# Turning the softmax rows by VectorE and a way through memory instead of by TensorE

## The chip, the cores and the metric

The kernel runs on one core of one Trainium2 chip. Its time is the device time of one execution in microseconds; a kernel's figure is the median of its runs. Beside the times there is one profiled execution, recorded instruction by instruction, from which all rows quoted here come. TensorE (PE, with its weight loads PEld) multiplies matrices, VectorE (DVE), ScalarE (ACT) and GpSimd (POOL) work on tiles, SyncE (SP) issues DMAs. The matrices pass through TensorE as float32r pairs: each operand is split into a high part and a low part (the rest), and a product is made of two or three matmuls.

## The reference, cut to what matters

One encoder block over 512 positions of width 2048. An adaLN-modulated RMSNorm gives `h`; one projection of `h` feeds 16 attention heads of width 64 and a gated linear attention (GLA); both are gated, concatenated and projected back.

```
h = rms_norm(x) * (1 + scale) + shift
proj = h @ w_in                       # q, k, v, gate of attention; q, k, v, gate, decay of GLA
for window, dilation in ((128, 1), (512, 4), (2048, 16)):
    s = q k^T / 8 + bias              # masked to the pattern
    o_p, lse_p = softmax(s) v, logsumexp(s)
att = sum_p softmax(lse)_p * o_p      # = one softmax over all positions, with a bias that counts
                                      #   how many patterns a pair of positions lies in
```

As the last comment says, the three patterns together are one softmax over the 512 keys with another bias, and that is how the kernel computes it: for each head and each tile of 128 queries a row block of scores 128 x 512, its softmax P, and P v. For P v TensorE needs P with the keys in the partitions, so P (queries in the partitions) has to be turned.

## The kernel before, in words

The weights stream through memory once, in groups of 512 KB (`fetch`, buffers `raw`), are split into parts by ScalarE (`split_hi`, L313) and VectorE (`split_lo`, L297), and are multiplied with `h` in *units* of 512 columns. A unit (`unit`) issues 64 steps ("ticks") of three matmuls each (L169 to L171, 512 columns wide): 8 weight groups of 8 ticks. Between the ticks stands side work, given as a list of pairs (place from 0 to 1, function); what has a place of 1 or more spills into the next unit. The order of TensorE's instructions is that of the program. The instructions of the other engines are laid into their queues by a scheduler, which looks at readiness and priority; each queue then runs strictly in its order.

Attention is side work of four units: qk2, qk4, qk6 and gk. Each takes four heads with four query tiles each, 16 score tiles (`attention`). For one tile `score` multiplies queries with keys (two matmuls, L576 and L577), VectorE adds the bias row and takes the minimum (L580), ScalarE exponentiates with a row sum (L583), VectorE inverts the sum (L584), GpSimd scales the row (L585). Two items later `turn` transposes the tile by four TensorE transposes into PSUM (L597), and ScalarE and VectorE read the high and the low part of P^T from there (L601, L602). When the two tiles of a half (256 queries) are turned, `values` makes eight matmuls with them (L611), ScalarE copies half of the result (L614) and VectorE adds the other (L618). At the end of each qk unit `qk_evict` moves the new queries and keys out of PSUM (L539 to L551), with DMAs that copy between partition halves.

Score tiles, softmax rows, queries and keys share 16 buffers of one kind (`T2`); the parts of P^T share eight larger ones (`B8`) with other tensors; PSUM tiles of attention share three banks (`PA`). The loads of weights use four buffers (`RAW`).

Two units of attention also carry `some_sums`: multiply-and-sum passes of VectorE over matrices that are loaded for that (L680, L244), which later units carry too.

Of the kernel before, what the change touches and what calls it, by code (L numbers as in the profile page):

```python
# [18 lines left out]
P = 128  # L19
# [50 lines left out]

ATT_AT = (0.17, 0.8, 0.04, 0.05, 0.05)

GLA_AT = (0.01, 0.02, 0.33, 0.46, 0.46, 0.56, 0.64, 0.76, 0.76, 0.88)
GLA_FIRST = 0.2

SUMS_IN = {"qk6": 4, "gk": 4, "gv0": 9, "gv1": 2, "ag0": 7, "ag1": 9, "gg0": 9}


def _plan(tasks, free, ready):
# [52 lines left out]
def block_kernel(ctx: ExitStack, tc: tile.TileContext, a: dict):  # L134
# [21 lines left out]
    def PA(name):  # L156
        return pp.tile([P, 512], F32, tag="pa", bufs=3, name=name)
# [47 lines left out]
    def RAW(name, shape):  # L205
        return wp.tile([P] + shape, F32, tag="raw", bufs=4, name=name)
# [349 lines left out]
    def attention(pairs):  # L556

        tiles = [(2 * p + j, i) for p in pairs for j in range(2) for i in range(4)]
        gt, pt, pr_ = {}, {}, {}
        heads = [2 * p + j for p in pairs for j in range(2)]  # L560

        def g_load(h):
# [4 lines left out]
        def score(h, i):  # L567
            def go():
                if h % 8 == 0 and i == 0:
                    cat[h // 8] = B8(f"cat{h // 8}", [4, 512])  # L570
                if i == 1 and h != heads[-1]:
                    g_load(h + 1)
                qs, ks, kl, _ = stacks[h]
                q = slice(P * i, P * i + P)
                ps = PA(f"s{h}{i}")
                mm(ps, qs[:, q], ks, start=True, stop=False)  # L576
                mm(ps, qs[:, q], kl, start=False, stop=True)  # L577
                t = T2(f"p{h}{i}")
                st = sm.tile([P, 3], F32, tag="st", name=f"st{h}{i}", bufs=6)
                nc.vector.tensor_tensor_reduce(  # L580
                    out=t, in0=ps, in1=gt[h][:, P * i:P * i + 512], op0=ALU.add, op1=ALU.min,
                    scale=1.0, scalar=3e38, accum_out=st[:, 0:1])
                act(t, t, AF.Exp, bias=st[:, 0:1], scale=-1.0, accum_out=st[:, 1:2])  # L583
                nc.vector.reciprocal(st[:, 2:3], st[:, 1:2])  # L584
                nc.gpsimd.tensor_scalar(t, t, st[:, 2:3], 1.0, op0=ALU.mult, op1=ALU.mult)  # L585
                pr_[h, i] = t
            return go

        def turn(h, i):
            def go():  # L590
                half, ii = divmod(i, 2)
                if ii == 0:
                    pt[h, half] = B8(f"pt{h}{half}", [2, 4, 256], F32R)
                t = pr_.pop((h, i))
                pk = PA(f"t{h}{i}")
                for kt in range(4):
                    nc.tensor.transpose(pk[:, kt * P:kt * P + P], t[:, kt * P:kt * P + P], ident)  # L597
                hi = pt[h, half][:, 0, :, P * ii:P * ii + P]
                lo = pt[h, half][:, 1, :, P * ii:P * ii + P]
                src = pk.rearrange("p (k q) -> p k q", k=4)  # L600
                act(hi, src, AF.Copy)  # L601
                tt(lo, src, hi.bitcast(F32), op=ALU.subtract)  # L602
            return go
# [16 lines left out]

        items = []
        n = len(tiles)
        for x in range(n + 4):
            if x < n:
                items.append(score(*tiles[x]))
            if 2 <= x <= n + 1:
                items.append(turn(*tiles[x - 2]))
            if 3 <= x <= n + 2 and tiles[x - 3][1] % 2 == 1:
                items.append(values(tiles[x - 3][0], tiles[x - 3][1] // 2))
        g_load(heads[0])  # L630
        start, span, move0, move1, move_last = ATT_AT
        at = [start + (q + 0.5) / len(items) * span for q in range(len(items))]
        at[0] -= move0
        at[1] -= move1
        at[-1] += move_last
        return list(zip(at, items))

    def gate_half(m, z):

# [203 lines left out]
    def unit(name, natural, side=(), rhs=None, lr=None, tiles=range(4)):  # L843
# [5 lines left out]
        for q in range(KT // 2):  # L849
# [3 lines left out]
            if 0 in tiles:  # L853
                todo = list(range(gi[name, gorder[0] if name == "o3" else 0], upto[name, g] + 1))
                for i in todo:
                    split_hi(i)
                for ahead in (1, 2):
                    fetch(upto[name, g] + ahead)
            if i0 not in low:
                split_lo(i0)  # L860
# [270 lines left out]
```

## Time and profile before

| | us |
|---|---|
| median of 3 runs | 958.21 |
| lowest, highest run | 958.14, 959.61 |
| profiled execution | 959.9 |
| its span in the trace | 957.9 |

The span is the time from the first to the last recorded instruction; 2.0 us of the execution lie around it. In the groups of instructions, a row names the line, the engine, the operation, the tiles written and read, the shapes and the count; then the busy time and the mean of one in ns; then how long the engine stood idle just before them, and what ended that. A helper's line stands for all that call it. In the answers in order of time, a row gives the start, the duration, the engine and the instruction, and in brackets the idle time before it. In the chain of work that ended last, a row gives the start, the time that the chain spent on the instruction, and the instruction; "issue" is time in which nothing recorded was waited for. In DMA rows stand the size of one and the median time from issue to landing.

### The profile page before, as it was taken

The page shows a single profiled execution, that of the slowest core. Times are in us where ns is not written, and L with a number is a line of the kernel's source. Part 1 is how long each engine was busy: PE and PEld are TensorE (multiplying, and loading weights), DVE is VectorE, ACT ScalarE, POOL GpSimd, SP SyncE. Part 2 cuts the span into 40 slices and gives each one's busy share as a digit, 9 for nine tenths or more (in the row PEclk, how much of TensorE's full clock was granted, in tenths as well). Part 3 has the DMA queues.
Part 4 walks back from the last instruction along what each step waited for, and adds up shares of the span by engine and source line. Part 5 has one row for each costly group of instructions (what it writes and reads, how often), then busy time and mean ns, then how long its engine had stood idle before and what let it go on. Part 6 is the DMA issues. An engine that isn't in the chain of part 4 may idle for free.

```text
span 957.9 us, 11999 instructions
## 1 busy us (share of the span) xinstructions
PE 939.7 (98%) x4464; PEld 777.1 (81%) x4464; DVE 605.3 (63%) x900; ACT 431.5 (45%) x719; POOL 81.1 (8%) x100
## 2 busy tenths in 40 slices
PE   8999999999999999999999999999999999999996
PEld 5888788888888888888778888888887888888884
DVE  7988899675756676766435656675964352546421
ACT  5443533565655655655215544543834152233222
POOL 0000000012122022122000000000010000202120
PEclk9999999999999999999999999999999999999998
DMA  9999687443333463533454244354555464244013
GB/s 330 413 411 365 229 296 275 150 131 105 112 103 105 144 200 108 173 127 103 150 176 146 86 132 154 132 176 154 173 195 183 132 221 154 92 151 152 23 55 121
DMA packets 45180, 163.76 MB, mean 171 GB/s; under 512 B 5730, under 2 KB 6018, under 8 KB 40386
## 3 DMA queue, kind: packets, MB, share of 16 engines
q1 hardware_dynamic: 44946, 162.68, 49.9%
q8 instruction: 35, 0.57, 0.2%
q10 hardware_dynamic: 176, 0.33, 0.1%
q14 instruction: 23, 0.18, 0.1%
HBM read 154.51 MB, written 4.28 MB: 166 GB/s over the span
## 4 chain that ended last, share of the span: by engine, by line
PE 84%; DMA 6%; DVE 5%; issue 3%; ACT 1%; SPq 0%; POOL 0%; ACTq 0%; DVEq 0%; POOLq 0%
PE ps_o L170 6%; PE ps_o L169 6%; PE ps_o L171 6%; DMA rawg<-in_wg 6%; PE ps_qk L170 5%; PE ps_qk L169 5%; PE ps_qk L171 5%; PE o L611 3%; PE sta L169 3%; PE sta L170 3%; PE sta L171 3%; PE stb L171 3%; PE stb L169 3%; PE stb L170 3%; PE ps_gv L171 3%; PE ps_gv L170 3%
## 5 line engine op out<-in xcount | busy, mean ns | idle before, releaser
L585 POOL TENSOR_SCALAR p<-p,st 128x512 f32<-128x512 f32 x64 | 45.5, 711 | 406.6 <-DVE st L584 357.9
L244 DVE CUSTOM_DVE_ANT_0 cb<-cb,sb,c_bcond 128x2048 f32<-128x2048 f32 (+1 forms) x32 | 73.4, 2294 | 0.0
L583 ACT ACTIVATE p<-p,st 128x512 f32<-128x512 f32 x64 | 46.1, 721 | 56.8 <-DVE st L580 56.3
L602 DVE TENSOR_TENSOR pt<-t,pt 128x512 fp32r<-128x512 f32 x64 | 44.0, 689 | 16.2 <-ACT pt L601 15.8
L580 DVE CUSTOM_DVE_ANT_0 p<-s,g 128x512 f32<-128x512 f32 x64 | 43.6, 687 | 14.8 <-PE s L577 14.5
L601 ACT ACTIVATE pt<-t 128x512 fp32r<-128x512 f32 x64 | 37.8, 592 | 10.2 <-PE t L597 9.2
L244 DVE CUSTOM_DVE_ANT_0 rawg<-rawg,sb,gate 128x1024 f32<-128x1024 f32 x16 | 20.5, 1283 | 29.6 <-DMA rawg<-in_wg 29.6
L611 PEld LDWEIGHTS o<-pt,vv 128*128 128x128 f32 x256 | 34.7, 188 | 5.0 <-DVE pt L602 2.2
L597 PEld LDWEIGHTS t<-c_ident,p 128*128 128x128 f32 x256 | 31.8, 140 | 8.5
L597 PE MATMUL t<-c_ident,p 128*128 128x128 f32 x256 | 38.3, 272 | 0.0
L611 PE MATMUL o<-pt,vv 128*128 128x256 f32 x256 | 36.6, 283 | 0.9 <-DVE pt L602 0.8
L244 DVE CUSTOM_DVE_ANT_0 rawg<-rawg,sb,c_bcond 128x1024 f32<-128x1024 f32 x16 | 20.5, 1283 | 26.3 <-DMA rawg<-in_wg 26.3
L1014 POOL TENSOR_TENSOR x<-x,fgain 128x512 f32<-128x512 f32 x12 | 20.3, 1696 | 185.3 <-ACT ysq L1012 185.3
L1012 ACT ACTIVATE ysq<-x 128x512 f32<-128x512 f32 x16 | 10.1, 632 | 47.2 <-DVE x L1010 47.2
L767 POOL TENSOR_SCALAR dc<-st,sc 128x256 f32<-128x256 f32 x16 | 10.4, 652 | 245.5 <-DVE st L764 240.6
L1009 DVE TENSOR_TENSOR y<-ps_o,sb 128x512 f32<-128x512 f32 x16 | 10.9, 684 | 25.9 <-PE ps_o L171 25.9
L584 DVE RECIPROCAL st<-st 128x1 f32<-128x1 f32 x64 | 10.3, 162 | 24.9 <-ACT p L583 24.9
L576 PE MATMUL s<-ks,qs 128*128 128x512 f32 x64 | 25.1, 391 | 0.0
L577 PE MATMUL s<-kl,qs 128*128 128x512 f32 x64 | 25.0, 391 | 0.0
L774 ACT ACTIVATE sq<-st,sc 128x256 f32<-128x256 f32 x24 | 12.2, 509 | 26.8 <-DVE st L769 14.3
L1010 DVE TENSOR_TENSOR x<-y,x 128x512 f32<-128x512 f32 x16 | 18.0, 1125 | 0.3
L614 ACT ACTIVATE oh<-o 64x256 f32<-64x256 f32 x32 | 12.2, 382 | 13.0 <-PE o L611 12.2
(1275 smaller groups left out, 2916.7 us busy)
## 6 DMA issues: line engine op xcount, KB each, us to landing
cb<-in_wm SPq DMA_DIRECT2D x31, 1024.0 KB, 7.9
rawg<-in_wg SPq DMA_DIRECT2D x32, 512.0 KB, 3.4
raw_o<-in_w_o SPq DMA_DIRECT2D x32, 512.0 KB, 3.4
raw_qk<-in_w_qk SPq DMA_DIRECT2D x24, 512.0 KB, 3.4
rawb<-in_w_sb SPq DMA_DIRECT2D x16, 512.0 KB, 4.8
rawv<-in_wv SPq DMA_DIRECT2D x16, 512.0 KB, 3.8
raw_gv<-in_w_gv SPq DMA_DIRECT2D x16, 512.0 KB, 3.5
raw_ag<-in_w_ag SPq DMA_DIRECT2D x16, 512.0 KB, 3.3
```

The source lines that it names most:

```text
L169: mm(ps, lh, rh, start=first, stop=False)
L170: mm(ps, ll, rh, start=False, stop=False)
L171: mm(ps, lh, rl, start=False, stop=last)
L244: nc.vector.tensor_tensor_reduce(out=w, in0=w, in1=with_, op0=ALU.mult, op1=ALU.add, scale=1.0, scalar=init, accum_out=dst)
L576: mm(ps, qs[:, q], ks, start=True, stop=False)
L580: nc.vector.tensor_tensor_reduce(out=t, in0=ps, in1=gt[h][:, P * i:P * i + 512], op0=ALU.add, op1=ALU.min, scale=1.0, scalar=3e38, accum_o ...
L583: act(t, t, AF.Exp, bias=st[:, 0:1], scale=-1.0, accum_out=st[:, 1:2])
L585: nc.gpsimd.tensor_scalar(t, t, st[:, 2:3], 1.0, op0=ALU.mult, op1=ALU.mult)
L597: nc.tensor.transpose(pk[:, kt * P:kt * P + P], t[:, kt * P:kt * P + P], ident)
L601: act(hi, src, AF.Copy)
L602: tt(lo, src, hi.bitcast(F32), op=ALU.subtract)
L611: mm(po[:, :256], vv[h // 4][:, kt, h % 4, :], t[:, w, kt, :], start=kt == 0 and w == 0, stop=kt == 3 and w == 1)
```

## The change

The four TensorE transposes of a score tile go. VectorE turns the tile in blocks of 32 x 32 into a new tile, with the blocks put in another order; a DMA writes that to memory (`away`, two tiles for a half); four DMAs read a half back, each into 32 partitions, in runs of 512 bytes, so that the keys lie in the partitions. The high and the low part of a half are then made by one instruction each from that buffer, which is of the same kind as the weights' (`RAW`). Scaling, turning, reading back, splitting and value products become list items of their own, placed 0.45, 1.05, 3.4, 5.6 and 7.2 tiles behind the scores; a tile is 0.0555 of a unit. The value products of the last halves of a unit thereby spill into the next. Weights are fetched one group ahead instead of two in these four units, and the sums that two of them carried move to later units.

```diff
-ATT_AT = (0.17, 0.8, 0.04, 0.05, 0.05)
+ATT_AT = (0.13, 0.0555)
...
-SUMS_IN = {"qk6": 4, "gk": 4, "gv0": 9, "gv1": 2, "ag0": 7, "ag1": 9, "gg0": 9}
+SUMS_IN = {"gv0": 12, "gv1": 5, "ag0": 8, "ag1": 9, "gg0": 9}
...
                 act(t, t, AF.Exp, bias=st[:, 0:1], scale=-1.0, accum_out=st[:, 1:2])
+                pr_[h, i] = t, st
+            return go
+
+        def scale(h, i):
+
+            def go():
+                t, st = pr_.pop((h, i))
                 nc.vector.reciprocal(st[:, 2:3], st[:, 1:2])
                 nc.gpsimd.tensor_scalar(t, t, st[:, 2:3], 1.0, op0=ALU.mult, op1=ALU.mult)
+                half, ii = divmod(i, 2)
+                if ii == 0:
+                    away[h, half] = dp.tile([2, P, 512], F32, tag=f"away{h}{half}", name=f"away{h}{half}")
                 pr_[h, i] = t
             return go
 
         def turn(h, i):
             def go():
                 half, ii = divmod(i, 2)
-                if ii == 0:
-                    pt[h, half] = B8(f"pt{h}{half}", [2, 4, 256], F32R)
-                t = pr_.pop((h, i))
-                pk = PA(f"t{h}{i}")
-                for kt in range(4):
-                    nc.tensor.transpose(pk[:, kt * P:kt * P + P], t[:, kt * P:kt * P + P], ident)
-                hi = pt[h, half][:, 0, :, P * ii:P * ii + P]
-                lo = pt[h, half][:, 1, :, P * ii:P * ii + P]
-                src = pk.rearrange("p (k q) -> p k q", k=4)
+                t = T2(f"pt{h}{i}")
+                nc.vector.transpose(t.rearrange("p (b k r) -> p k b r", b=4, k=4), pr_.pop((h, i)))
+                nc.sync.dma_start(away[h, half][ii], t)
+            return go
+
+        def back(h, half):
+
+            def go():
+                t = away.pop((h, half))
+                f = RAW(f"pf{h}{half}", [8, 128])
+                for b in range(4):
+                    nc.sync.dma_start(f[32 * b:32 * b + 32], bass.AP(
+                        t.tensor, t.offset + P * b, [[512, 32], [32 * 512, 8], [1, P]]))
+                pf[h, half] = f
+            return go
+
+        def parts(h, half):
+            def go():
+                t = pt[h, half] = B8(f"pt{h}{half}", [2, 4, 256], F32R)
+                src = pf.pop((h, half)).rearrange("p b (k r) -> p k b r", k=4)
+                hi, lo = [t[:, e].rearrange("p k (b r) -> p k b r", b=8) for e in range(2)]
                 act(hi, src, AF.Copy)
                 tt(lo, src, hi.bitcast(F32), op=ALU.subtract)
             return go
...
-        for x in range(n + 4):
-            if x < n:
-                items.append(score(*tiles[x]))
-            if 2 <= x <= n + 1:
-                items.append(turn(*tiles[x - 2]))
-            if 3 <= x <= n + 2 and tiles[x - 3][1] % 2 == 1:
-                items.append(values(tiles[x - 3][0], tiles[x - 3][1] // 2))
+        for x in range(n):
+            if True:
+                items.append((x, score(*tiles[x])))
+                items.append((x + 0.45, scale(*tiles[x])))
+                items.append((x + 1.05, turn(*tiles[x])))
+                if tiles[x][1] % 2 == 1:
+                    h, half = tiles[x][0], tiles[x][1] // 2
+                    items.append((x + 3.4, back(h, half)))
+                    items.append((x + 5.6, parts(h, half)))
+                    items.append((x + 7.2, values(h, half)))
+        items.sort(key=lambda v: v[0])
         g_load(heads[0])
...
+        start, step = ATT_AT
+        return [(start + step * x, go) for x, go in items]
...
-                for ahead in (1, 2):
+                for ahead in (1, 2)[:1 if name[:2] in ("qk", "gk") else 2]:
                     fetch(upto[name, g] + ahead)
...
-        ps = unit(n, False, attention((p, p + 1)) + ([(0.05, shift_row)] + some_sums(n) if p == 4 else []))
+        ps = unit(n, False, attention((p, p + 1)) + ([(0.05, shift_row)] if p == 4 else []))
...
-    ps = unit("gk", False, attention((6, 7)) + some_sums("gk"))
+    ps = unit("gk", False, attention((6, 7)))
```

More of the change, by code (lines that the diff above doesn't have):

```diff
@@ L558, in attention @@
         tiles = [(2 * p + j, i) for p in pairs for j in range(2) for i in range(4)]
-        gt, pt, pr_ = {}, {}, {}
+        gt, pt, pr_, away, pf = {}, {}, {}, {}, {}
         heads = [2 * p + j for p in pairs for j in range(2)]
@@ L622, in attention @@
         n = len(tiles)
-        for x in range(n + 4):
-            if x < n:
-                items.append(score(*tiles[x]))
-            if 2 <= x <= n + 1:
-                items.append(turn(*tiles[x - 2]))
-            if 3 <= x <= n + 2 and tiles[x - 3][1] % 2 == 1:
-                items.append(values(tiles[x - 3][0], tiles[x - 3][1] // 2))
-        g_load(heads[0])
[L631 to L636, printed above, removed]
+        for x in range(n):
[9 more added lines that the diff above has]
+        items.sort(key=lambda v: v[0])
+        g_load(heads[0])
+        start, step = ATT_AT
+        return [(start + step * x, go) for x, go in items]
     def gate_half(m, z):
```

## The prediction

> **What bounds the kernel now.** I read the totals first, then a table of the four stretches in which attention runs, then the chain of work that ended last, then single instructions in order of time.
>
> ```profile
> PE 939.7 (98%) x4464; PEld 777.1 (81%) x4464; DVE 605.3 (63%) x900; ACT 431.5 (45%) x719; POOL 81.1 (8%) x100
> ...
> 200.00:264.00 64.00, 63.97 (x343) 53.87 (x342) 41.37 (x88) 36.49 (x72) 11.15 (x16) 1.00 0.37 112
> 264.00:330.00 66.00, 65.97 (x352) 55.45 (x351) 41.95 (x88) 37.61 (x73) 11.17 (x16) 1.00 0.36 108
> 330.00:400.00 70.00, 69.97 (x369) 58.83 (x369) 50.06 (x104) 38.41 (x74) 11.13 (x16) 1.00 0.53 166
> 400.00:460.00 60.00, 59.16 (x322) 49.84 (x321) 39.03 (x86) 34.31 (x68) 12.05 (x16) 1.00 0.38 123
> ```
>
> The columns of the table are the stretch, its length, busy time and instructions of PE, PEld, DVE, ACT and POOL, the granted clock, the DMA share and GB/s. TensorE has no gap worth naming in these 260 us; VectorE has 20 us or more free in each stretch, the DMA engines half their time. So TensorE's queue sets the time here, and an instruction taken off it is worth its place in that queue. The chain gives the place:
>
> ```profile
> 204.04 0.23 PE ps_qk L171
> 204.27 0.44 PE t L597 x4
> ...
> 210.68 0.94 PE o L611 x8
> ...
> 455.15 0.44 PE t L597 x4
> ```
>
> A 512-column matmul takes 0.23 us, the four transposes of a score tile 0.44, the eight value products of a half (two score tiles) 0.94. The transposes' own durations in the groups (256 of 272 ns) overlap and are not the price.
>
> One thing more is to be seen in the old kernel: what happens when an engine in front of a value product works through other things first.
>
> ```profile
> 449.51 1.22 DVE L297 TENSOR_TENSOR gv01l<-raw_gv,gv01h 128x1024 fp32r<-128x1024 f32 x1
> 450.72 1.27 DVE L244 CUSTOM_DVE_ANT_0 rawv<-rawv,shb,vbias 128x1024 f32<-128x1024 f32 x1
> 451.54 0.28 PE L611 MATMUL o<-pt,vv 128*128 128x256 f32 x1
> 452.65 0.74 PE L611 MATMUL o<-pt,vv 128*128 128x256 f32 x4 [0.84 <-DVE pt L602]
> ```
>
> The first product reads the high part and runs at 451.54; the second needs the low part, which VectorE makes only after two unrelated instructions, and TensorE stands 0.84 us. Queues are in order: what stands ahead in VectorE's queue is TensorE's wait.
>
> **The change part by part.** I write s62 for the score products of head 6, query tile 2; exp62 and score62 for what ScalarE and VectorE do with it; high41, low41 and o41 for the two parts and the value products of the second half of head 4.
>
> *Transposes off TensorE.* 64 tiles x 0.44 = 28.2 us saved, all of it on the path.
>
> *Work on the other engines.* Per half VectorE loses two low parts from PSUM and ScalarE two high parts; they get one each of 128x1024, and VectorE two turns of 128x512.
>
> ```profile
> L602 DVE TENSOR_TENSOR pt<-t,pt 128x512 fp32r<-128x512 f32 x64 | 44.0, 689 | 16.2 <-ACT pt L601 15.8
> L601 ACT ACTIVATE pt<-t 128x512 fp32r<-128x512 f32 x64 | 37.8, 592 | 10.2 <-PE t L597 9.2
> L717 DVE TENSOR_TENSOR_SCAN b<-rst,g 128x512 f32<-128x512 f32 x4 | 4.9, 1225 | 0.1
> ```
>
> No row shows a 32-block turn by VectorE. The nearest are passes over 128x512: 0.69 us at the low end, the scan's 1.23 at the high end; I take 0.69, the ordinary pass with one input and one output. Per unit (16 tiles) VectorE changes by -16 x 0.69 + 8 x 1.23 (the row below) + 16 x 0.69 = +10 us, to about 52 of the 58 us that TensorE would need (65 less 7); with 1.23 it would be 60, and VectorE the bound by 2 us a unit. That is not yet the main thing. The Trainium skill ("VectorE: DVE Perf Modes", The three transpose paths) gives 311 ns for a 128x128 bf16 turn; four would be an estimated 1.24 us, no run here shows it, and by it the sum below would be 5 us higher.
>
> *The order, where the loss lies.* By program order the parts stand 1.6 tiles ahead of the values, but the queues of VectorE and ScalarE are laid by a scheduler. As the changed kernel is built, they run, around o41:
>
> ```
> TensorE: s62, 3 projection matmuls, o41, 9 projection matmuls, s63
> VectorE: score62, turn61, reciprocal62, low41, weights' low part, add41, score63
> ScalarE: exp61, exp62, high41, weights' high part, copy41, exp63
> ```
>
> high41 comes behind exp62, which needs score62, which needs s62: TensorE is asked for o41 three matmuls after s62, and the parts cannot be begun before s62 has gone through two engines. The durations of this chain:
>
> ```profile
> 200.63 0.69 DVE L580 CUSTOM_DVE_ANT_0 p<-s,g 128x512 f32<-128x512 f32 x1
> 201.37 0.73 ACT L583 ACTIVATE p<-p,st 128x512 f32<-128x512 f32 x1 [2.13 <-DVE st L580]
> 203.20 0.39 PE L577 MATMUL s<-kl,qs 128*128 128x512 f32 x1
> 203.63 0.69 DVE L580 CUSTOM_DVE_ANT_0 p<-s,g 128x512 f32<-128x512 f32 x1 [0.54 <-PE s L577]
> 204.36 1.06 ACT L313 ACTIVATE qk24h<-raw_qk 128x1024 fp32r<-128x1024 f32 x1 [1.47 <-issue]
> 205.32 0.71 ACT L583 ACTIVATE p<-p,st 128x512 f32<-128x512 f32 x1
> 205.45 1.23 DVE L297 TENSOR_TENSOR qk24l<-raw_qk,qk24h 128x1024 fp32r<-128x1024 f32 x1 [1.13 <-ACT qk24h L313]
> 206.15 0.60 ACT L601 ACTIVATE pt<-t 128x512 fp32r<-128x512 f32 x1
> 206.78 0.69 DVE L602 TENSOR_TENSOR pt<-t,pt 128x512 fp32r<-128x512 f32 x1
> ```
>
> From the start of the second score product: 0.43 to the score pass (203.20 to 203.63), 0.74 to the exponential (200.63 to 201.37), 0.83 to ScalarE's next (205.32 to 206.15), the high part 1.06, 0.03 to VectorE (206.75 to 206.78), the low part 1.23, and 0.04 to TensorE (taken as the same hand-over): 4.36 us. TensorE has 4 x 0.23 = 0.92 of work in that time. Stall: 3.44 us.
>
> I went through all 32 halves in this way. For those at a unit's end the queries and keys are evicted between:
>
> ```profile
> L548 ACT ACTIVATE ks<-ps_qk 64x512 fp32r<-64x512 f32 x12 | 7.1, 593 | 3.8 <-DVE kl L550 3.2
> L550 DVE TENSOR_TENSOR kl<-ps_qk,ks 64x512 fp32r<-64x512 f32 x12 | 8.3, 689 | 0.9 <-ACT ks L548 0.6
> L618 DVE TENSOR_TENSOR cat<-o,oh 64x256 f32<-64x256 f32 x32 | 13.3, 416 | 7.3 <-ACT oh L614 6.8
> L584 DVE RECIPROCAL st<-st 128x1 f32<-128x1 f32 x64 | 10.3, 162 | 24.9 <-ACT p L583 24.9
> L585 POOL TENSOR_SCALAR p<-p,st 128x512 f32<-128x512 f32 x64 | 45.5, 711 | 406.6 <-DVE st L584 357.9
> ```
>
> - 7 halves as o41 (o31, o41, o70, o71, o81, o111, o121): 7 x 3.44 = 24.1.
> - o30 and o110: reciprocal and low part also wait for a weight's low part: score 0.74, turn 0.69, weights 1.23, reciprocal 0.16 make 2.82 where 2.66 stood: 2 x 3.6 = 7.2.
> - o11, o51, o91, o131 follow their score directly, with 0.23 of cover: 4 x 4.13 = 16.5.
> - o10, o50, o90, o130: the chain starts one score earlier, 15 x 0.23 = 3.45 of cover: 4 x 0.91 = 3.6.
> - o01: only the low part is behind, score and turn ahead of it: 0.43 + 0.74 + 0.69 + 1.23 + 0.04 - 0.92 = 2.2.
> - o20, o60, o100: two evictions of 0.59 more on ScalarE, 13 x 0.23 of cover: 4.36 + 1.18 - 2.99 = 2.55, three times 7.7.
> - o21, o61, o101: VectorE has five evictions of 0.69, weights 1.23, add 0.42, turn 0.69, low part 1.23 between the two low parts, with the hand-over 7.06; TensorE has 0.94 + 23 x 0.23 = 6.23: 3 x 0.83 = 2.5.
> - o140: reciprocal, Pool's scaling and turn153 come first: 0.43 + 0.74 + 0.83 + 0.16 + 0.71 + 0.69 + 1.23, with hand-overs 4.9; less 2.99: 1.9.
> - o00, o40, o80, o120 and o141: no stall; their parts stand ahead of the score that counts.
>
> Together 65.7 us. The wait is TensorE's, and behind it in its queue stand the next projection matmuls, so nothing hides it.
>
> *The way through memory.* Per half two writes of 256 KB and four reads of 64 KB in runs of 512 bytes, issued by SP, whose queue also carries the weights.
>
> ```profile
> 195.54 0.46 SPq L551 DMA_DIRECT2D kl<-kl  x1
> ...
> raw_qk<-in_w_qk SPq DMA_DIRECT2D x24, 512.0 KB, 3.4
> ...
> out<-x SPq DMA_DIRECT2D x16, 256.0 KB, 2.6
> ks<-ks SPq DMA_DIRECT2D x16, 128.0 KB, 2.2
> ...
> c_ident<-in_ident SPq DMA_DIRECT2D x1, 64.0 KB, 4.2
> ```
>
> About 7.5 issues of 0.46 = 3.5 us in the 9 us of a half (75 a unit, eight halves). A read is issued some two score tiles (over 6 us) ahead of its high part in nearly all halves, against 2.2 to 4.2 us of landing plus 1.4 for four issues: hidden. The slack is thinnest at o30, o70, o110 (about 1 us) and in the spilled halves o150 and o151, whose reads wait for a buffer that the half before gives back; for those I add 2 us together (bounds 0 and 6). Weights are now fetched one group ahead instead of two; a group lasts 7 us or more. SP waits for a turn before each write, and a weight load stands behind it; the turn is always well ahead of the need.
>
> *Sums moved.* Eight leave the attention units, where VectorE had room and nothing was saved; three each go to two later units, one each to two more. 1.28 us of VectorE each, covered there while TensorE has its 43 us of projection: 0, bounds 0 and 6.
>
> *The sum.* -28.2 + 65.7 + 2 = +39.5. The profiled execution took 959.9 us (span 957.9 and 2.0 around it), 1.7 above the median of 958.2: 999.4 as profiled, 998 as a median.
>
> **The rivals.**
>
> *Clock.* A matmul of the start runs cold:
>
> ```profile
> 13.69 0.63 PE L169 MATMUL sta<-sa0h,h_hi 128*128 128x512 f32 x1
> 14.12 0.63 PE L170 MATMUL sta<-sa0h,h_lo 128*128 128x512 f32 x1
> 17.32 0.39 PE L169 MATMUL sta<-sa0h,h_hi 128*128 128x512 f32 x1
> ```
>
> 0.43 apart until about 17, then 0.23: 5 us that are worth 2.4. If each stall of 3.4 us or more (13) brought this back: +31, 1029. No gap that long lies in the warm part of this trace, and each stall here is broken by one product. The Trainium skill ("TensorE: Matmul & The Clock Gate", Why this matters for your kernels) asks for no idle gap above about 3 us, which speaks for this rival. Chance 0.10 (1010 to 1035).
>
> *The round trip is late.* If the four reads land 2 us after the high part is due in half of the 32 halves, +32: 1030 (1015 to 1060). For it: runs of 512 bytes, and weights in the same queues; against it: the DMA share of 0.4. Chance 0.06.
>
> *Short runs crawl.* 64 KB in 512-byte rows took 4.2 us to land, 512 KB of weights 3.4. If that were a rate and not a latency, the four reads of a half would take 16.8 us one after the other, 32 halves 538 us where four units of 75 make 300: +240, 1200. For it: the two rows. Against it: keys of 128 KB landed in 2.2 us, and the 4.2 is a single copy among weight loads. 0.02. The Trainium skill warns in the section named above that a plain copy with strides as a transpose is 19 times slower than a transposing one where the innermost stride is large; it speaks against this change, but here the innermost run is 512 bytes long.
>
> *Faster: TensorE stays the bound.* If the parts are made ahead of the score that the values follow, the stalls vanish and only the 28.2 remain: 930. For it: VectorE and ScalarE have the time. It decides at 28.2 / 32 = 0.88 us of stall a half; my count gives 2.1. Against it: the built order, and the 0.84 us above. Chance 0.10. Half the stalls would come out even: 0.03.
>
> **How the numbers follow.** The forecast has 0.69, with a range of its own of 984 to 1014 (turn at 1.23: +5; parts on split patterns some tenths slower in 25 halves: +8; the memory's bounds and the sums: -2 to +10; hand-overs 0.2 us shorter or a half judged wrong: -12). The range 978 to 1036 takes in the clock and the nearer part of the late round trip, and leaves out the rest. Faster 0.10, within 0.2% (about what a measurement of this kernel can tell) 0.03, slower 0.87.
>
> **What would show it.** Right: no L597 on TensorE; PE's waits headed by the value products waiting for the low part of pt, some 25 of them and 2 to 4 us long, 60 us in all; the high parts idle for "DVE st" or nothing, not for DMA; units of 75 us or more where 66 stood. Wrong: value products without waits (930), high parts that wait for pf's DMA (round trip), matmuls 0.43 apart after a stall (clock), or a turn that takes over 1.5 us.

## The result and the profile after

| | before | after |
|---|---|---|
| median of 4 runs | 958.17 | 1029.22 |
| lowest, highest run | 957.88, 959.61 | 1024.92, 1030.30 |
| profiled execution | 959.9 | 1024.9 |
| its span | 957.9 | 1023.0 |

The ratio is 1.073 (95% interval 1.0697 to 1.0763): 71 us slower. The forecast was 998, the range 978 to 1036. The totals of the page after, with TensorE's granted clock in 40 slices:

```profile
PE 945.2 (92%) x4208; PEld 771.3 (75%) x4208; DVE 642.0 (63%) x932; ACT 425.6 (42%) x687; POOL 80.6 (8%) x100
...
PEclk9999999999899879989999999999999999999999
```

The 256 transposes are gone (4464 matmuls before, 4208 now), yet TensorE is busy 5.5 us longer. Without them, 939.7 - 28.2 = 911.5 us were to be expected: the same matmuls took 33.7 us more. TensorE's idle time, span less busy time, went from 18.2 to 77.8 us. So the profiled span changed by -28.2 + 33.7 + 59.6 = +65.1 us. The four stretches in the table of stretches (length, then busy time and instructions of PE, PEld, DVE, ACT and POOL, granted clock, DMA share, GB/s):

```profile
200.00:264.00 64.00, 55.68 (x245) 45.23 (x244) 43.02 (x88) 29.43 (x55) 12.10 (x16) 0.95 0.64 181
264.00:330.00 66.00, 55.12 (x240) 44.34 (x240) 37.81 (x77) 25.69 (x47) 9.16 (x14) 0.92 0.71 196
330.00:400.00 70.00, 53.70 (x211) 41.95 (x211) 38.08 (x70) 27.62 (x49) 7.95 (x12) 0.83 0.63 174
400.00:460.00 60.00, 45.93 (x189) 36.49 (x188) 35.03 (x64) 25.10 (x44) 8.01 (x11) 0.87 0.66 183
```

Where TensorE was busy without a gap at full clock, it now does 885 matmuls in these 260 us instead of 1386 (256 of them the transposes), with gaps, and at 0.83 to 0.95 of the clock. VectorE is busy 35 to 43 us and ScalarE 25 to 29 us of each stretch: neither became the bound. TensorE's waits (line waited for, total, times, longest):

```profile
PE o L635 <- ACT pt L625: 27.8, 14, 2.6
PE o L635 <- DVE pt L626: 18.3, 21, 1.7
PE ps_qk L169 <- ACT qk62h L313: 4.0, 1, 4.0
PE ps_qk L169 <- ACT qk42h L313: 3.2, 1, 3.2
...
PE ps_gk L169 <- ACT gk2h L313: 2.6, 1, 2.6
PE ps_gk L170 <- DVE gk2l L297: 2.2, 1, 2.2
```

46.1 us go to the two parts of the turned rows, in 35 waits, where the old kernel had 0.8. Another 13.5 us go to parts of weights at the starts of three units (the four rows here and 1.5 us in shorter ones); these had not been expected. Around o41, in order of time:

```profile
310.76 0.39 PE L577 MATMUL s<-kl,qs 128*128 128x512 f32 x1
...
313.74 0.38 PE L635 MATMUL o<-pt,vv 128*128 128x256 f32 x1 [1.91 <-ACT pt L625]
315.00 1.82 PE L635 MATMUL o<-pt,vv 128*128 128x256 f32 x7 [0.88 <-DVE pt L626]
316.62 0.63 PE L169 MATMUL ps_qk<-h_hi,qk45h 128*128 128x512 f32 x1
...
318.64 0.39 PE L171 MATMUL ps_qk<-h_lo,qk45h 128*128 128x512 f32 x1
...
311.19 0.69 DVE L580 CUSTOM_DVE_ANT_0 p<-s,g 128x512 f32<-128x512 f32 x1 [0.75 <-PE s L577]
...
313.72 1.23 DVE L626 TENSOR_TENSOR pt<-pf,pt 128x1024 fp32r<-128x1024 f32 x1 [0.78 <-DMA g<-grow]
...
311.93 0.72 ACT L583 ACTIVATE p<-p,st 128x512 f32<-128x512 f32 x1 [1.68 <-DVE st L580]
...
312.64 1.04 ACT L625 ACTIVATE pt<-pf 128x1024 fp32r<-128x1024 f32 x1
```

Score, exponential, high part, low part follow one another in the order of the forecast, and TensorE stands twice. (The releaser named for the low part, g, is none of its operands; the part started 0.04 us after the end of ScalarE's high part.) Then comes the second loss: the matmuls from 316.62 on start 0.43 us apart, from 318.64 on 0.23.

The rows of the new work, and of its DMAs (KB, median us to landing):

```profile
L626 DVE TENSOR_TENSOR pt<-pf,pt 128x1024 fp32r<-128x1024 f32 x32 | 38.9, 1216 | 17.5 <-ACT pt L625 13.2
L605 DVE STREAM_TRANSPOSE pt<-p 128x512 f32<-128x512 f32 x64 | 45.3, 708 | 4.8 <-POOL p L592 4.2
L625 ACT ACTIVATE pt<-pf 128x1024 fp32r<-128x1024 f32 x32 | 33.4, 1045 | 4.5 <-DMA pf<-away 3.7
...
away<-pt SPq DMA_DIRECT2D x64, 256.0 KB, 2.2
pf<-away SPq DMA_DIRECT2D x128, 128.0 KB, 4.2
...
raw_qk<-in_w_qk SPq DMA_DIRECT2D x24, 512.0 KB, 4.1
```

### The profile page after: what moved, and what is told of

Same layout as the page of the kernel before. It is cut to its first block, busy times and chain, and to the rows that moved or that the text cites. A ratio compares the mean times of both kernels' runs of the same rounds, so it can differ in the third digit from the quotient of the medians.

```text
span 1023.0 us, 11804 instructions
## 1 busy us (share of the span) xinstructions
PE 945.2 (92%) x4208; PEld 771.3 (75%) x4208; DVE 642.0 (63%) x932; ACT 425.6 (42%) x687; POOL 80.6 (8%) x100
## 4 chain that ended last, share of the span: by engine, by line
PE 72%; DMA 9%; DVE 7%; ACT 4%; issue 4%; SPq 3%; POOL 0%; ACTq 0%; DVEq 0%; POOLq 0%
PE ps_o L170 6%; PE ps_o L171 6%; PE ps_o L169 6%; DMA pf<-away 3%; PE sta L169 3%; PE sta L170 3%; PE sta L171 3%; PE ps_ag L171 3%; PE stb L171 3%; PE ps_ag L169 3%; PE ps_ag L170 3%; PE stb L170 3%; PE stb L169 3%; PE o L635 2%; PE ps_gg L171 2%
## 5 line engine op out<-in xcount | busy, mean ns | idle before, releaser
L635 PE MATMUL o<-pt,vv 128*128 128x256 f32 x256 | 50.1, 334 | 46.2 <-ACT pt L625 27.8
L635 PEld LDWEIGHTS o<-pt,vv 128*128 128x128 f32 x256 | 40.7, 222 | 59.3 <-ACT pt L625 34.5
L626 DVE TENSOR_TENSOR pt<-pf,pt 128x1024 fp32r<-128x1024 f32 x32 | 38.9, 1216 | 17.5 <-ACT pt L625 13.2
L605 DVE STREAM_TRANSPOSE pt<-p 128x512 f32<-128x512 f32 x64 | 45.3, 708 | 4.8 <-POOL p L592 4.2
L625 ACT ACTIVATE pt<-pf 128x1024 fp32r<-128x1024 f32 x32 | 33.4, 1045 | 4.5 <-DMA pf<-away 3.7
L642 DVE TENSOR_TENSOR cat<-o,oh 64x256 f32<-64x256 f32 x32 | 13.2, 414 | 21.1 <-ACT oh L638 20.6
```

The source lines that it names most:

```text
L605: nc.vector.transpose(t.rearrange("p (b k r) -> p k b r", b=4, k=4), pr_.pop((h, i)))
L635: mm(po[:, :256], vv[h // 4][:, kt, h % 4, :], t[:, w, kt, :], start=kt == 0 and w == 0, stop=kt == 3 and w == 1)
```

## The experiments

All runs in one table; us, from each kernel's profiled execution except for the median and the ratio to the kernel before. "Parts" is TensorE's wait for pt, "starts" its waits for weights' parts and for the eviction of queries and keys (nearly all at units' starts), "longer" is busy time less 911.5 less 0.2275 for each added matmul.

| run | median | ratio (95%) | parts | starts | longer | clock |
|---|---|---|---|---|---|---|
| after | 1029.2 | 1.0697 to 1.0763 | 46.1 | 13.5 | 33.7 | 0.966 |
| e1_fill | 1022.4 | 1.0625 to 1.0686 | 19.8 | 16.8 | 14.9 | 0.986 |
| e11_fill_half | 1026.2 | 1.0677 to 1.0729 | 30.5 | 16.2 | 30.3 | 0.968 |
| e2_pinned | 982.4 | 1.0208 to 1.0271 | 2.3 | 25.1 | 19.0 | 0.975 |
| e3_later | 1022.2 | 1.0595 to 1.0702 | 29.5 | 28.4 | 29.6 | 0.972 |
| e4_before_sums | 961.7 | 1.0003 to 1.0039 | 1.2 | 0 | - | 0.998 |
| e5_pinned_g | 983.4 | 1.0238 to 1.0273 | 14.1 | 15.2 | 19.0 | 0.974 |
| e6_pinned_g_pool | 968.2 | 1.0080 to 1.0124 | 15.0 | 9.7 | 11.0 | 0.982 |
| e7_pinned_g_pool_two | 965.8 | 1.0048 to 1.0104 | 14.6 | 9.9 | 6.5 | 0.987 |
| e8_unpinned_g_pool | 989.0 | 1.0305 to 1.0337 | 34.8 | 7.2 | 16.5 | 0.980 |
| e9_queues | 951.8 | 0.9923 to 0.9948 | 4.1 | 14.3 | 4.9 | 0.991 |
| e10_queues_early | 964.7 | 1.0047 to 1.0089 | 3.4 | 13.9 | 6.7 | 0.985 |
| e12_evict_order | 957.5 | 0.9976 to 1.0016 | 1.7 | 14.7 | 11.5 | 0.981 |

Three theories stood against each other for the 71 us: the order of parts behind scores (the forecast), a clock that goes cold in the gaps, and transfers or SyncE's queue that come late.

### The clock: gaps filled (e1) and half filled (e11)

```diff
+    FILL = {(1, 1): 12, (5, 1): 12, (9, 1): 12, (13, 1): 12, (2, 0): 6, (6, 0): 6, (10, 0): 6}
+    for q in ((3, 0), (3, 1), (4, 1), (7, 0), (7, 1), (8, 1), (11, 0), (11, 1), (12, 1)):
+        FILL[q] = 10
...
                 po = PA(f"o{h}{half}")
+                for _ in range(FILL.get((h, half), 0)):
+                    mm(po, h_hi[:, 0, :P], h_hi[:, 1, :], start=True, stop=True)
```

For e11 the counts are 6, 3 and 5 instead of 12, 6 and 10.

> The changed kernel with dummy products of TensorE (high parts of h, 512 columns, into the PSUM tile that the value products then overwrite) put ahead of the value products of the 16 halves with the longest waits: 12 in four of them, 10 in nine, 6 in three, 156 in all, each 0.22 us warm; nothing else is changed. Theory (the cold clock is a second loss of some 30 us beside the waits, set off by idle time of TensorE of 2.6 us and more): the granted clock of the whole run rises from 0.966 to 0.985 or more, the runs of matmuls 0.43 us apart go where a gap was filled, the remaining waits for low parts fall below half of the 46 us, and the time falls by 15 to 30 us, to 1000 to 1015, though TensorE is given 35 us more to do. Rival (the clock is lost to the work itself, not to the gaps; the loss is the waits alone): the dummies only fill time that is lost anyway, the clock stays near 0.966 and the time at 1025 to 1035.

> The changed kernel with dummy products as in the first run, but half as many (6, 5 and 3 in the same 16 halves: 78 products, 17 us where they lie on the path), so that they cover about half of a wait instead of more than it. Theory (the first run's 156 products were 8 us longer than the waits that they filled, and the cold clock costs some 30 us of which it won back half): the waits for pt fall to about 29 us, what is left of each long wait is near 1.3 us and sets off no slow stretch, granted clock 0.983 to 0.99, time 1010 to 1019, below the first run's 1022. Rival (only a queue without any gap keeps the clock): granted clock as in the unfilled kernel, 0.966 to 0.972, and 1025 to 1032.

With the full filling the waits fell by 26 us, TensorE's longer busy time by 19 and the clock rose to 0.986, but the time only by 7, to 1022.4: 156 products are 35.5 us, more than the waits that they filled. The theory holds for the clock, and its time (1000 to 1015) was wrong by the size of the filling. For e11 the theory failed and the rival held: half the filling took a third of the waits away and the clock stayed at 0.968. The reason is in the rows. The same half, o11, first in e1, then in e11:

```profile
245.17 2.88 PE L637 MATMUL o<-h_hi 128*128 128x512 f32 x12
247.98 0.38 PE L640 MATMUL o<-pt,vv 128*128 128x256 f32 x1
249.24 1.10 PE L640 MATMUL o<-pt,vv 128*128 128x256 f32 x7 [0.88 <-DVE pt L629]
250.17 0.40 PE L169 MATMUL ps_qk<-h_hi,qk27h 128*128 128x512 f32 x1
```

```profile
245.30 1.52 PE L637 MATMUL o<-h_hi 128*128 128x512 f32 x6
248.10 0.39 PE L640 MATMUL o<-pt,vv 128*128 128x256 f32 x1 [1.28 <-ACT pt L628]
249.36 1.18 PE L640 MATMUL o<-pt,vv 128*128 128x256 f32 x7 [0.87 <-DVE pt L629]
250.34 0.63 PE L169 MATMUL ps_qk<-h_hi,qk27h 128*128 128x512 f32 x1
```

A wait of 0.88 us alone left the matmuls behind it fast; 1.28 and 0.87 us with one product between them were followed by seven matmuls 0.43 us apart. Between 200 and 510 us, 13 halves of the changed kernel had two waits in a row, and a slow stretch followed 11 of them; in e11 8 of 12, down to pairs of 0.77 and 0.88 us; in e1, where at most 0.24 us of the first wait was left, no half brought one. What decides is idle time within a fixed stretch of 3.41 us; the last section shows it.

### The order of parts and scores (e2), and more cover behind the score (e3)

```diff
+    last = {}
+
+    def behind(ins, key):
+        if key in last:
+            tc.add_manual_dep(ins.ins, last[key], mybir.DependencyInfo(
+                mybir.DependencyClass.NoSync, mybir.DependencyReason.DATA), reason="order")
...
-                nc.vector.tensor_tensor_reduce(
+                i_s = nc.vector.tensor_tensor_reduce(
...
-                act(t, t, AF.Exp, bias=st[:, 0:1], scale=-1.0, accum_out=st[:, 1:2])
+                i_e = act(t, t, AF.Exp, bias=st[:, 0:1], scale=-1.0, accum_out=st[:, 1:2])
+                behind(i_s, "lo")
+                behind(i_e, "hi")
...
-                act(hi, src, AF.Copy)
-                tt(lo, src, hi.bitcast(F32), op=ALU.subtract)
+                last["hi"] = act(hi, src, AF.Copy).ins.name
+                last["lo"] = tt(lo, src, hi.bitcast(F32), op=ALU.subtract).ins.name
```

> The changed kernel with two orders pinned and no instruction added: on VectorE each bias-and-minimum pass (L580) follows the low part that the program made last before it, on ScalarE each exponential (L583) the high part made last before it. In the built order the parts now stand one to two score tiles ahead of their value products, instead of behind the score that comes next to them. Theory (the queues' order makes the waits): the waits for pt (27.8 and 18.3 us) fall to under 8 us together, the waits at the units' starts (13 us) stay, the granted clock goes to 0.985 or more, and the time falls by 60 to 85 us, to 940 to 970. Rival (the way through memory is late): the high part waits for the data that come back, VectorE and ScalarE stand with the next score behind it, TensorE waits for scores instead, and the time stays over 1000.

No instruction was added or taken away, and 47 us went. TensorE's waits in e2:

```profile
PE plr L956 <- DVE lrs L949: 5.3, 1, 5.3
PE ps_qk L169 <- ACT qk62h L313: 4.7, 1, 4.7
PE ps_qk L169 <- DVE qs L540: 4.4, 3, 2.0
...
PE o L643 <- DVE pt L634: 2.0, 3, 0.7
```

The waits for parts fell from 46.1 to 2.3 us, as the theory has it, so the order makes them. The rival is out for the inner halves: ScalarE waited 12.5 us for data that came back, and TensorE did not see it. The time stayed 12 us above the theory's 970, because the waits at the starts grew from 13.5 to 25.1 us (16.5 for weights, and now 8.6 for the eviction of queries and keys), one wait for the small weights lrs behind gk grew from 1.1 to 5.3 us, and the clock stayed at 0.975.

```diff
-                    items.append((x + 7.2, values(h, half)))
+                    items.append((x + 7.6, values(h, half)))
```

> The changed kernel with the value products 7.6 tiles behind their scores instead of 7.2: three more projection matmuls, six or nine in some halves, run between the score and the products, so 0.7 to 2 us more cover for each half; the products stand later than the parts by that much, the queues of VectorE and ScalarE are otherwise the same in kind. Theory (the cover after the score is short): the waits for pt fall by 20 us and more of 46, the granted clock rises to 0.98 or more, time 985 to 1008. Rival (the parts are laid later too, or the data come back late): waits as before, 1020 to 1035.

The waits for parts fell by 17 us, those at the starts grew by 15, and the time by 7 (1015 to 1028 in single runs): what the halves gained was given back at the next unit's start, into which later products spill. The theory's mechanism is seen, its sum failed.

### The side parts of the change (e4)

```diff
-SUMS_IN = {"qk6": 4, "gk": 4, "gv0": 9, "gv1": 2, "ag0": 7, "ag1": 9, "gg0": 9}
+SUMS_IN = {"gv0": 12, "gv1": 5, "ag0": 8, "ag1": 9, "gg0": 9}
...
-                for ahead in (1, 2):
+                for ahead in (1, 2)[:1 if name[:2] in ("qk", "gk") else 2]:
```

As in the change, the calls of `some_sums` in qk6 and gk go too.

> The kernel before with only the side parts of the change: the sums of qk6 and gk moved to gv0, gv1 and ag0, and weights fetched one group ahead instead of two in the qk and gk units; turning stays on TensorE. By the prediction these cost nothing (moved sums 0, bounds 0 to 6; fetch one ahead 0): 958 plus or minus 2. Rival: the later fetch is late for the splits at the units' starts, where the changed kernel lost 13 us to parts of weights: 965 to 975.

The median is 2.9 us above, a little outside the forecast of 956 to 960; the ratio of 1.0021 makes it 2.0. By themselves these parts cost next to nothing.

### SyncE's queue (e5, e6, e8)

What delays the starts is seen in SyncE's queue of the changed kernel, in order of time:

```profile
255.75 0.34 SPq L606 DMA_DIRECT2D away<-pt  x1
...
260.77 0.46 SPq L551 DMA_DIRECT2D kl<-kl  x1
266.14 0.34 SPq L606 DMA_DIRECT2D away<-pt  x1
...
269.01 0.58 SPq L564 DMA_DIRECT2D g<-grow  x1
269.63 1.86 SPq L286 DMA_DIRECT2D raw_qk<-in_w_qk  x1
```

From 260.77 to 266.14 SyncE issued nothing: it stood in front of a write for its turn, and behind that write were the keys' copies, the bias rows and the weights that TensorE missed at 277. Over the run it waited for turns in front of writes 153.7 us.

```diff
-                if i == 1 and h != heads[-1]:
+                if i == 1 and h < 15:
...
-        g_load(heads[0])
+        if heads[0] == 0:
+            g_load(0)
```

> The kernel with the pinned orders, and the bias rows (g) of a unit's first head loaded during the last head of the unit before, as they are for the other heads, instead of at the unit's start. At the start of qk4 in the pinned run g was issued at 262.5 and VectorE waited 5.6 us for it with the first exponential queued before the first weights' high part on ScalarE; three such waits sum to 15.7 us. Theory (g at the end of SyncE's queue is what is late at the units' starts): those 15.7 us of VectorE's waits go, TensorE's waits of 11.5 us for qk42, qk62 and gk2 fall below 4 us, and with the cold clock behind them (granted clock 0.975) the time falls by 15 to 25 us, to 957 to 967. Rival (the weights themselves land late, since they are issued after the copies of keys and away-writes): the waits for g go, those for the weights' high parts stay near 10 us, and the time falls by 0 to 6 us.

TensorE's wait for qk62 went with those for g, gk2's fell to 0.6 us, and the time did not change (982.4, 983.4). The rival holds: the weights are late themselves. At the start of qk6 ScalarE stood 8.98 us for the load of qk62, and the high part of a half was queued behind it, so that TensorE's wait for the weights became one of 8.20 us for that half's products. In e6 also the writes left SyncE:

```diff
-                nc.sync.dma_start(away[h, half][ii], t)
+                nc.gpsimd.dma_start(away[h, half][ii], t)
```

> As the run before, and the writes of turned tiles (away) issued from GpSimd's queue instead of SyncE's, where 59 of them held the queue for 118 us waiting for a turn. Theory (SyncE's queue behind a turn delays keys and weights): the copies ks and kl and the weights of the next unit are issued sooner, and TensorE's waits at the three units' starts (qs, kl, qk42, qk62, gk2: 23 us in the pinned run) fall below 8 us together: 945 to 958. Rival (the DMA engines are full there, busy 0.8 to 1.05 in the slices around the starts): issued sooner, they land no sooner, and the time is that of the run before within 4 us; if GpSimd's queue is held by the write in front of the next scaling, slower by up to 10.

15 us less than e5, so SyncE's queue is a loss of its own. The DMA engines take back a part of the sooner issue: a group of weights now lands 6.0 us after it instead of 4.1, and the time falls all the same. e8 has the edits of e5 and e6 without the pinned orders:

> The changed kernel without pinned orders, with only the bias rows loaded a unit ahead and the writes of turned tiles issued by GpSimd. Tells the units' starts apart from the order of parts and scores. Theory (both are losses of their own): waits for pt stay at 40 us or more, the waits at the starts (13.5 us) fall by 8 us or more, and the time is 1029 less 10 to 20: 1009 to 1019. Rival (the starts are late only because the units before ended behind): nothing changes, 1024 to 1034.

40 us, twice what the theory allowed. This run doesn't separate what it should: with the writes on another engine the scheduler laid the queues anew, and in the built order high41 now stands ahead of exp61, so part of the 40 us is the order again (parts 34.8 instead of 46.1). Against e6 the pinned orders are worth 21 us in these queues, where they were worth 47 in those of the changed kernel.

### What is left: a version that beats both (e7, e9, e10, e12)

```diff
-                for ahead in (1, 2)[:1 if name[:2] in ("qk", "gk") else 2]:
+                for ahead in (1, 2):
...
-            qk_evict(p + 2 + q, ps[2 * q], ps[2 * q + 1])
+            with tc.high_priority(offset=20):
+                qk_evict(p + 2 + q, ps[2 * q], ps[2 * q + 1])
```

> As the run before, with weights fetched two groups ahead in these units as in the kernel before the change, and the eviction of new queries and keys given the priority of attention's steps. Theory (one group ahead is too short beside the traffic of the turned tiles, whose loads make weights land in 4.3 us instead of 3.4): the waits for weights' parts go, the granted clock reaches 0.99, time 930 to 948. Rival (four buffers are shared with the data that come back: what weights take ahead, those wait for): the waits move to the value products or to the scores, and the time is no better than the run before, 945 to 965.

2 us, within the spread of the runs: the theory failed, and the waits stayed at the value products (14.6 us). Two of the halves that spill over a unit's end still kept TensorE for 9.5 and 2.3 us. The longer one in TensorE's and ScalarE's rows of e7:

```profile
336.84 0.58 PE L644 MATMUL o<-pt,vv 128*128 128x256 f32 x1 [9.48 <-ACT pt L634]
...
334.79 1.06 ACT L313 ACTIVATE qk63h<-raw_qk 128x1024 fp32r<-128x1024 f32 x1 [8.99 <-DMA raw_qk<-in_w_qk]
```

The high part comes right behind the split of qk63, whose weights SyncE had asked for at 328.85, after the copies of the keys. e9 takes out of SyncE's queue what stood there:

```diff
-            nc.sync.dma_start(ks[oth].bitcast(F32), ks[own].bitcast(F32))
+            nc.scalar.dma_start(ks[oth].bitcast(F32), ks[own].bitcast(F32))
...
-            nc.sync.dma_start(kl[oth].bitcast(F32), kl[own].bitcast(F32))
+            nc.scalar.dma_start(kl[oth].bitcast(F32), kl[own].bitcast(F32))
...
-        ps = unit(n, False, attention((p, p + 1)) + ([(0.05, shift_row)] if p == 4 else []))
+        ps = unit(n, False, attention((p, p + 1)))
...
-    ps = unit("gk", False, attention((6, 7)))
+    ps = unit("gk", False, attention((6, 7)) + [(0.5, shift_row)])
```

> The kernel of the run before last but one (pinned orders, bias rows a unit ahead, writes from GpSimd, weights two ahead, eviction urgent), with the copies of keys (ks, kl) issued by ScalarE right behind what makes them, and the 1 MB load of the shift row (shb, used only by the moved sums) moved from the start of qk6 to the middle of gk. There, at 319 to 330, SyncE stood with the key copies, each waiting for an eviction, and the data of the last halves were asked for only at 329.7; TensorE waited 9.5 us for them at 336.8 and 2.3 us at the start of qk4. Theory (the last halves' way through memory stands in SyncE's queue behind the key copies): those waits of 12 us go with some 6 us of cold clock, the evictions' waits of 10 us stay: 940 to 954, so faster than the kernel before by 5 to 18 us. Rival (the DMA engines themselves, or the four buffers shared with weights, are late): waits at the starts as before, 960 to 968.

951.8 us, 0.65% below the kernel before (0.9923 to 0.9948) and 77 us below the changed one. TensorE's waits that remain, in the profiled execution, which with 955.8 us was the longest of six:

```profile
PE ps_qk L169 <- DVE qs L540: 6.8, 4, 2.1
PE ps_gk L169 <- DVE qs L540: 4.0, 2, 2.0
...
PE o L644 <- ACT pt L634: 1.5, 2, 1.3
```

The two waits of together 12 us are gone, as the theory has it; those for evictions did not stay at 10 but grew to 14.3. The theory named only the returned data as late; the rows above show the weights as well, and both were asked for behind the keys' copies. Which of the two edits did how much wasn't separated.

```diff
-                    items.append((x + 3.4, back(h, half)))
+                    items.append((x + 2.4, back(h, half)))
```

> As the run before, with the data of a half asked for one tile sooner (2.4 tiles behind the scores instead of 3.4). If the data are late, the waits of ScalarE for pf (9.5 us in the last run) fall and the time is up to 6 us lower than the run before; if the four buffers are what is short, holding one of them a tile longer makes the weights late and the time is 2 to 10 us higher.

13 us slower than e9. ScalarE waited less for pf (10.0 us instead of 23.4), so the first sentence holds, but TensorE stood 10.4 us once, where e9 has 1.8, for the small weights lrs of the next unit: their load was issued at 456.95, behind reads that held SyncE, instead of 449.42. That one wait is 8.6 of the 9.3 us between the two profiled executions (955.8 and 965.1); the buffers were not looked at apart from it.

In e12 the last exponential of a unit is pinned on ScalarE behind the second eviction of queries (L540 there):

```diff
+                if i == 3 and h == heads[-1]:
+                    last["end"] = i_s, i_e
...
+        if "end" in last:
+            for late, first_ in list(zip(last.pop("end"), (q_lo, q_hi)))[1:]:
+                tc.add_manual_dep(late.ins, first_.ins.name, mybir.DependencyInfo(
+                    mybir.DependencyClass.NoSync, mybir.DependencyReason.DATA), reason="order")
```

> The best kernel so far (951.8) with one more order pinned: on ScalarE the last exponential of a unit behind the two evictions of new queries that free the first PSUM bank. There TensorE waits 14 us at the three units' starts for these evictions, whose second one stood on ScalarE behind that exponential (1.34 us idle for its minimum) and a copy of value products. Theory (this order is late): 4 to 8 us of those waits go, with some cold clock: 942 to 949. Rival (as built, the split of weights now comes between the two evictions, 1.06 us on ScalarE and 1.23 on VectorE, and takes the place): 950 to 955.

957.5: the rival, and a little worse. The first wait at a start is now 3.49 us instead of 1.97, with the split of qk42 (1.04 on ScalarE, 1.23 on VectorE) between the two evictions. The 14 us of evictions stay open.

## Why the prediction was right in its sign and 31 us low

- **"All of it on the path" (-28.2).** Right: the transposes are gone, and where the waits and the cold clock are taken away (e9), the time falls below the kernel before, by 6 of the 28. Most of the rest is in e9's row: 14.3 and 4.1 us of waits and 4.9 of longer busy time.
- **The turn taken as 0.69 us.** Measured 0.708. The estimate of 1.24 from the Trainium skill ("VectorE: DVE Perf Modes", The three transpose paths) is not borne out for this shape and type. VectorE is no bound.
- **"The order, where the loss lies" (65.7 us).** The mechanism is shown by e2. The size was too large: 46.1. For halves like o41 the trace has 1.91 + 0.88 = 2.79 where 3.44 stood; the chain took 4.24 us instead of 4.36, and the first product (0.38), which runs between the two waits, had been counted as waiting. For o11 and its like 3.52 instead of 4.13, for o20 2.46 instead of 2.55, for o10 0.62 instead of 0.91. o21, o61, o101 didn't wait, nor did o110; o30 waited 0.53. Why the halves next to a unit's start waited less than counted was not taken apart. The signs fit in part: 35 waits of up to 2.64 us, not 25 of 2 to 4, headed by the high part (27.8), not the low; three units took 85 to 92 us, but the first 63.
- **"The turn is always well ahead of the need".** This step failed. SyncE stood 153.7 us in front of writes for turns, and weights behind them came late at the starts, where TensorE waited 13.5 us for their parts (in e8 all waits at the starts are 7.2); with pinned orders the writes alone are worth 15 us (e6). With the o-waits the idle time came to +59.6, near the 65.7 + 2 of the sum, but from other places than it said: that is luck.
- **The way through memory, hidden (+2).** Right: ScalarE's high parts waited 3.7 us for pf in all. With the order pinned ScalarE waited 12.5 us for it and TensorE hardly, but for 2.3 us at a spilled half in e7. The 8 to 9.5 us at other spilled halves (e5, e7) are the weights' in front.
- **One group ahead, and the moved sums (0, bounds 0 and 6).** Right: 2 us (e4).
- **The clock (0 in the sum, chance 0.10, +31).** This term was mis-sized, and it is most of the difference between 998 and 1029: 33.7 us of longer busy time were measured, against the rival's 31. The forecast's own range, 984 to 1014, was missed; 1029 lies in the stated one because that took in this rival, and that the rival's sum gave 1029 too is luck, since it rested on 65.7 us of stalls. The argument against it was that each stall is broken by one product. The runs show that one product between does not help: 0.77 and 0.88 us around one product were enough in e11, because idle time adds up within a stretch of 3.41 us (last section). The Trainium skill ("TensorE: Matmul & The Clock Gate", Why this matters for your kernels) warns of gaps above about 3 us; here the longest single wait for a part was 2.64 us, so by that rule the clock would have stayed warm behind the halves, and the measurement decides against it. Some 27.9 of the 33.7 us are the clock (last section); the matmul beside a wait also counts 0.39 instead of 0.23.
- **Late round trip, short runs that crawl, faster.** None came: the high parts were not held by data, the reads land in 4.2 us, and no version reached 930. The four reads of a half are of 128 KB each (the row of pf above), not of 64 as the prediction has them; they landed in the 4.2 us that its copy of 64 KB took, so that this time was no rate.

## What to carry to other kernels

Before work is moved off a full engine, look at what each in-order queue will hold between the value that is needed and the instruction that makes it: here the order of two instructions was worth 47 us (21 once the writes had left SyncE) and an engine's instructions 28. A DMA that waits for a late producer belongs on a queue with nothing urgent behind it. Price a TensorE stall with the slow matmuls after it, and add up the idle time that falls into one stretch of 3.41 us.

## What the hardware showed that was not expected

What cools TensorE's clock is idle time within one fixed stretch of 3.41 us, in one wait or in two. In all fourteen traces the granted clock is 1.00 or 0.50, and within a trace all its changes lie a multiple of 3.41 us apart. Two stretches of this grid in the changed kernel, around o41 (columns as in the table of stretches; idle time is the length less PE's busy time):

```profile
311.66:315.07 3.41, 0.63 (x3) 0.26 (x2) 2.37 (x6) 2.71 (x4) 0.69 (x1) 1.00 1.05 328
315.07:318.48 3.41, 3.41 (x12) 3.02 (x13) 1.42 (x2) 0.38 (x1) 0.00 (x0) 0.50 0.91 263
```

TensorE is idle for 2.78 us of the first stretch, and the second runs at half the clock, the matmuls 0.43 us apart. Between 40 and 560 us the changed kernel has 14 stretches at full clock with 1.98 us of idle time or more, and each was followed by one at half; of the 119 with 1.72 us or less none was. Over all fourteen traces the border lies between 1.60 and 1.92 us, where both happened. The clock came back after a stretch with 0.52 us of idle time or less, and not after one with 0.58 or more. The 19 stretches at half clock hold 55.8 us of TensorE's busy time, half of which, 27.9 us, is an estimate of what the clock cost.

So the same two waits can do it or not. Two halves of e11, the waits and then the stretches:

```profile
293.00 0.38 PE L640 MATMUL o<-pt,vv 128*128 128x256 f32 x1 [0.77 <-ACT pt L628]
294.26 1.59 PE L640 MATMUL o<-pt,vv 128*128 128x256 f32 x7 [0.88 <-DVE pt L629]
...
382.29 0.39 PE L640 MATMUL o<-pt,vv 128*128 128x256 f32 x1 [0.78 <-ACT pt L628]
383.55 1.10 PE L640 MATMUL o<-pt,vv 128*128 128x256 f32 x7 [0.87 <-DVE pt L629]
...
291.20:294.61 3.41, 1.76 (x9) 1.06 (x8) 2.06 (x4) 2.80 (x4) 0.69 (x1) 1.00 0.87 288
294.61:298.02 3.41, 3.41 (x13) 2.93 (x12) 1.55 (x2) 0.38 (x1) 0.00 (x0) 0.50 0.80 217
...
379.94:383.36 3.42, 1.96 (x8) 1.14 (x7) 2.38 (x5) 2.35 (x4) 0.69 (x1) 1.00 0.91 283
383.36:386.77 3.41, 3.22 (x17) 2.83 (x18) 1.77 (x3) 0.86 (x2) 0.00 (x0) 1.00 0.99 223
```

The first pair lies in one stretch, 1.65 us of idle time; the second is cut by a border into 1.46 and 0.19 us. The single wait of 1.73 us in the changed kernel (o01, up to 230.94) was cut too, and left the clock alone; a single wait of 1.97 us in e9, at the start of qk6 within one stretch, halved it. The Trainium skill ("TensorE: Matmul & The Clock Gate", Part 1: The HAM clock gate) describes a free-running window of some 3.4 us. The traces agree with its length; the 1.6 to 1.9 us of idle time that suffice within it are this case's measurement.
